# Even mixer: 64-row and 32-row tiles of the array in place of masked keys, and heads handled in pairs

## The chip, the cores and the metric

The kernel runs as one program on one core of one Trainium2 chip. The metric is the device time of one execution in microseconds (us). PE is the matrix engine (PEld its weight loads), DVE the vector engine, ACT the scalar engine, POOL the general engine, SP the engine that issues most DMAs. Each engine works through its own list of instructions in order.

## The reference, cut to what matters

Two blocks are computed on 256 tokens of width 1024 in float32: a first block of two layers, then a second block whose first layer is the *even mixer* (on 256 latent and 256 context tokens), followed by 16 experts, a second mixer and experts again. The change lies in the even mixer:

```python
q_a = rms_norm(heads_a(aq), na_qg) * HD_A ** -0.5          # 8 heads of 64
o_a = neighbourhood_attention(q_a, k_a, v, ck_a, cv_a, rpb) # latents: window + all context
co_a = block_attention(cq_a, ck_a, cv_a)                    # context queries: context keys
# mLSTM: 4 heads, keys and queries of 64, values of 128, once forward and once backward
Dm = where(causal, b_i - b_j + i_j, NEG);  m = max(a, Dm.max(-1))
h  = (exp(Dm - m) * (q k^T)) v / max(|den|, exp(-m))
out = concat([o_a, norm(h_f + h_b) * sigmoid(mo)]) @ w_out
```

## The kernel before, in words

All weight products are made exactly in float32 from two float32r parts (a high and a low one): three products of 128x128 by 128x256 for one, named `pt` (token-major) or `pf` (feature-major). ACT and DVE split each weight block of 1 MB into its parts (`wh`, `wl`). Small products (attention, transposes) run in float32; the profile records each of those as two instructions. PE's tile shape stands in the profile as rows*columns: 128*128 is the whole array, 64*128 its upper or lower half of rows, 128*64 one half of its columns.

The order of every engine's list is set before the run by a planner, from priorities, expected times and the time at which tiles come free. Tiles lie in pools beside each other in memory; the pools of the even mixer reuse the first block's memory, and a tile of the new pool can be written only when what lay there has been read.

The end of the first block: four chunks of the output product (`pt<-w,yT`), the squares of each chunk (`fjunk`, ACT), their sum (`fsum`, DVE), then on POOL 1/rms (`fnr`) and the 1/rms of the result (`fn2r`), `x<-xf` on DVE and ACT, and two diagonal matrices (`cT`). The even mixer needs its input feature-major: for the context tokens squares (`xn<-xc`), 1/rms (`nrme`, `nrmr` on POOL), diagonals `cT`, then eight blocks `htp` (PE) to `hfull` (ACT) to `hT`, `hTl` (DVE); for the latent tokens the same eight blocks from `fn2r`. Every `pt<-w,hT` needs them.

In the even mixer four mLSTM heads come first: `cmb` spreads the running maxima over the partitions (K = 64 rows, of which one counts), ACT makes the weights `E0` (forward) and `E1` (backward), `qk` is q k^T, DVE multiplies it in, `pom` is the product with v. The planner fills PE's waits there with the `pt` of the first four neighbourhood heads. Then `na_pair` runs for two pairs of heads, another `na_qkv` and the output gate follow, and `na_pair` for two more. In `na_pair`, `lgN` and `lgC` are logits, DVE finds minima and adds the bias, ACT makes exponentials, DVE divides, PE transposes (`ntp`), `poN` is the product with v, 64 columns of the array at a time. Two heads of 64 lie on the 128 partitions of one block of q and k. Since a product contracts all 128 partitions, the key tiles `mk` and `nkT` hold every head apart, with zeros on the other head's 64 partitions.

The PSUM tag `lg` (`cmb`, `qk`, `lgN`, `lgC`) has two buffers, `tp` two, `po` one. The pools of the even mixer lie in the order evenA0, evenA (which holds `mk`), evenC (`wmg`, then `xn`, `cT`, `hfull`, `nkT`, `cm`), evenB, evenD.

Of the kernel before, what the change touches and what calls it, by code (L numbers as in the profile page):

```python
# [10 lines left out]
F32 = mybir.dt.float32  # L11
# [48 lines left out]
# ---------------------------------------------------------------- constants of the shapes  # L60
# [174 lines left out]
class Emit:  # L235
# [29 lines left out]
    # ------------------------------------------------------------ small helpers  # L265
# [7 lines left out]
    def warm(self, where, tag="lg", after=None):  # L273
        """products that nothing reads, behind the latest one traced: they keep the tensor engine's clock up while it waits"""
# [62 lines left out]
    def stream(self, units):  # L337
        """units: weight blocks [128, 8, 256] in DRAM in the order of their use; each step yields one as the exact
        sum of two float32r parts, and has the next one split already"""
        nc = self.nc  # L340
        for n, u in enumerate(list(units) + [None] * AHEAD):
            if u is not None:
                h, lo = (self.ring.tile([P, KD, UW], F32R, tag=tag, name=tag, bufs=RING[tag]) for tag in ("wh", "wl"))
                w = self.ring.tile([P, KD, UW], F32, tag="w", name="w", bufs=RING["w"])
                # the first ones in pieces: nothing else can run yet
# [11 lines left out]
    def split(self, hi, lo, src, eng="v"):  # L357
        """src -> hi + lo exactly, both float32r"""
        self.nc.scalar.copy(hi, src)  # L359
        (self.nc.vector if eng == "v" else self.nc.gpsimd).tensor_tensor(out=lo, in0=src, in1=hi.bitcast(F32), op=ALU.subtract)  # L360

    def mm3(self, out, a, b):
        """out = sum over k of a_k^T b_k for lists of pairs (hi, lo) of float32r parts: the product of the two low
        parts lies below the last bit of float32"""
# [7 lines left out]
    def diag(self, r, d):  # L372
        """column r [128, 1] -> d: the diagonal matrix of it"""
        self.affine(d, self.cst["ident"], r, eng="s")
        return d

    def rms_diag(self, x, junk, d):
        """x [128, 1024] token-major -> d: the diagonal matrix of 1 / rms of its rows"""
# [9 lines left out]
    def features(self, xs, ds, hT, A, B=None, tok0=0, pool=None):  # L388
        """token tiles xs (list of [128, 1024] APs) scaled by the diagonal matrices ds -> A_k * x^T + B_k as the sum of
        hT[0] and hT[1] [128, k, tok0...]"""  # L390
# [16 lines left out]
    def features1(self, x, d, hT, A, B, tok0, pool):  # L407
        """features of one token tile, four blocks of columns at a time"""
# [12 lines left out]
    # ------------------------------------------------------------ set up  # L421
# [36 lines left out]
    # ------------------------------------------------------------ first block  # L458
# [26 lines left out]
    def proj_feat(self, w, hT, c0=0, nb=2, ntok=S, width=P, b0=0):  # L485
        """feature-major product: psum [width, nb * ntok] for the columns c0.. of the unit w"""
# [8 lines left out]
    def proj_tok(self, w, hT, t0=0, ntile=2):  # L495
        """token-major product: psum [128, ntile, 256] for the token tiles t0.."""
# [8 lines left out]
    def silu2(self, ps, pool, g):  # L505
        """psum -> g: 2 * silu"""
# [6 lines left out]
    def softmax_rows(self, nl, n, bias, pool, tag, bufs=3):  # L513
        """nl psum [128, n] negated logits (bias already negated, or None): returns exp tile and its row sums"""
# [15 lines left out]
    def p_transposed(self, p0, p1, pool):  # L530
        """p0 [128, 128], p1 [128, 256] -> sbuf [128 keys, (k0: q 0..255 | k1: q 128..255)]"""
# [12 lines left out]
    def first_layer(self, l, pool):  # L544
# [21 lines left out]
        # ---- latents, index weights, rope key, index key  # L566
# [45 lines left out]
        # ---- index queries, diff queries  # L612
# [8 lines left out]
        # ---- index scores and top 64  # L621
# [32 lines left out]
        # ---- MLA q, k, v  # L654
# [23 lines left out]
        # ---- diff keys, dsa queries  # L678
# [10 lines left out]
        # ---- diff and dsa values, MLA gate  # L689
# [8 lines left out]
        # ---- MLA attention  # L698
# [25 lines left out]
        # ---- dsa keys  # L724
# [7 lines left out]
        # ---- differential attention  # L732
# [53 lines left out]
        # ---- diff and dsa gates  # L786
# [17 lines left out]
        # ---- DSA attention  # L804
# [24 lines left out]
        # ---- short convolution  # L829
# [19 lines left out]
        # ---- out  # L849
# [8 lines left out]
    def final_squares(self, pool, c):  # L858
        """chunk c of x times the gain, and the sums of squares of both"""
# [13 lines left out]
    def final_norm(self):  # L873
        """x <- x / rms * gain; 1 / rms of the result goes to self.r2"""
# [33 lines left out]
    # ------------------------------------------------------------ modulation vectors  # L908
# [12 lines left out]
    def ada_chunks(self, pool):  # L921
        """the modulation products, 2048 columns at a time; yields after each quarter of such a product"""
# [28 lines left out]
    def mod_cols(self, l):  # L951
        """feature-major columns of shift and scale of the mixer: A [128, 2, 8], B [128, 2, 8] (lat, ctx)"""
# [13 lines left out]
    def router_prep(self, l, pool, tag):  # L966
        """router weights times the scale of the expert input, and what its shift adds to the logits"""
# [20 lines left out]
    def out_proj(self, yT, targets, pool, rwA):  # L988
        """targets: (first token tile of yT, [128, 2, 1024] to add to, gate tile, 0 for latents or 1 for context).
        The router's products of the new tokens and their squares are gathered on the way"""  # L990
# [30 lines left out]
    def head_norm(self, ps, nh, dh, pool, tag):  # L1021
        """psum [128, nh*dh] token-major -> sbuf, each head divided by its rms"""
# [11 lines left out]
    # ------------------------------------------------------------ even mixer  # L1034
    def even_mixer(self, l):
        nc, io, cst = self.nc, self.io, self.cst
        NT = 4
        with ExitStack() as ctx:
# [18 lines left out]
            # neighbourhood bias, negated, with the window  # L1057
# [3 lines left out]
            def bias_half(g):  # L1061
                G2r = T([P, 4, 6, 64], "nkT")
                for rr in range(2):
                    # [63 - qc, head, d, kc] -> head*465 + (5 + d - rr)*31 + 15 + kc - qc
# [14 lines left out]
            # ---- mLSTM v  # L1079
# [10 lines left out]
            # ---- gates  # L1090
# [61 lines left out]
            # ---- mLSTM q, k  # L1152
            mq = T([P, 2, 512], "mq")
            mk = T([P, 2, 2, 512], "mk")
# [5 lines left out]
            for b in range(2):  # L1160
                ps = self.proj_feat(w, hT, c0=b * P, nb=1, ntok=512)
                nc.vector.tensor_tensor(mk[:, b], ps[:, None].to_broadcast([P, 2, 512]),
                                        cst["gm2"].unsqueeze(2).to_broadcast([P, 2, 512]), op=ALU.mult)
            bias_flip(1, G2r)

            # ---- NA q, k, v of four heads
            # ---- mLSTM
# [5 lines left out]
            def eoff(d, t, i):  # L1173
                """column of block (tokens j in tile t, tokens i in tile i) in the packed weights"""
# [10 lines left out]
            for h in range(4):  # L1185
                b, j = h // 2, h % 2
                E = []
                for d in range(2):
                    ps = self.psum("lg", name="cmb")
                    self.mm(ps, cst["ident"][:64, 32 * d + h:32 * d + h + 1].to_broadcast([64, P]), cm, True, True)  # L1190
                    Ed = T([P, 10 * P], f"E{d}")
                    for t in range(NT):
# [3 lines left out]
                        # keep where token j <= i (forward) or j >= i (backward); j on partitions  # L1196
# [4 lines left out]
                for t in range(NT):  # L1201
                    lo = 0 if t < 2 else 256
                    ps = self.psum("lg", name="qk")
                    self.mm(ps[:, lo:512], mk[:, b, j, t * P:(t + 1) * P], mq[:, b, lo:512], True, True)
# [22 lines left out]
            def na_qkv(tags):  # L1227
                nkT = T([P, 2, 2, 512], tags[1])
                nc.gpsimd.memset(nkT[0:64, :, 1], 0.0)
                nc.gpsimd.memset(nkT[64:128, :, 0], 0.0)  # L1230
# [12 lines left out]
                for t in range(0, NT, 2):  # L1243
# [5 lines left out]
                    tv = tp.rearrange("p (t b s) -> p t b s", t=2, b=2)  # L1249
                    for j in range(2):  # L1250
                        pr = slice(64 * j, 64 * j + 64)
                        self.affine(nkT[pr, :, j, t * P:(t + 2) * P].rearrange("p b (t s) -> p t b s", t=2), tv[pr],
                                    self.vcol("nak")[pr], eng="vs"[j])
# [6 lines left out]
            # ---- output gate of the mLSTM  # L1260
# [8 lines left out]
            # ---- neighbourhood attention  # L1269
            def na_pair(hp, nqT, nkT, nv):  # L1270
                hb = hp % 2
                po = self.psum("po", name="poN")
                for j in range(2):
                    h = 2 * hp + j
                    # latent queries
                    PT = T([P, 4, 2, P], f"E{j}")
                    for qt in range(2):
                        ps = self.psum("lg", name="lgN")
                        self.mm(ps, nqT[:, hb, 256 + qt * P:256 + (qt + 1) * P], nkT[:, hb, j], True, True)
# [3 lines left out]
                        bias = G2[:, h, 2 - 2 * qt:6 - 2 * qt].rearrange("p a b -> p (a b)")  # L1283
# [3 lines left out]
                        sm = self.sm.tile([P, 1], F32, tag="smx", name="smx", bufs=8)  # L1287
                        nc.scalar.activation(p, ps, AF.Exp, bias=mn, scale=-1.0, accum_out=sm)
                        r = self.sm.tile([P, 1], F32, tag="smr", name="smr", bufs=8)
                        nc.vector.reciprocal(r, sm)  # L1290
                        nc.vector.tensor_scalar(p, p, r, None, op0=ALU.mult)
# [3 lines left out]
                        self.copy(PT[:, :, qt], tp.rearrange("p (a s) -> p a s", a=4))  # L1295
                    for kt in range(4):
                        self.mm(po[64 * j:64 * j + 64, 256:512], nv[:, kt, (2 * hb + j) * 64:(2 * hb + j + 1) * 64],
                                PT[:, kt].rearrange("p a s -> p (a s)"), kt == 0, kt == 3)
                    # context queries
                    PC = T([P, 2, 2, P], f"E{j}")  # L1300
# [768 lines left out]
```

## Time and profile before

| what | value |
| --- | --- |
| median of 3 runs | 1570.04 us (1568.9 to 1570.42) |
| profiled execution, span | 1568.5 us, mean granted PE clock 0.958 |
| PE busy in it | 1427.8 us (91%) |
| DVE, ACT, POOL busy | 719.7, 441.2, 161.6 us |
| even mixer, from the first `htp<-cT,xc` to the last `poN` | 417 to 700 us |

The profiled execution shows no time beside its span; the span lies 1.5 us under the median of the runs. Busy time of PE includes the tail of each pipelined product, so the starts of successive products tell PE's pace better than their durations.

### The profile page before, as it was taken

Reading aid. Unit: us, or ns where it says so; the run is one execution under the profiler, and the core shown is the slowest. Engines: PE = TensorE matmul, PEld = TensorE weight load, DVE = VectorE, ACT = ScalarE, POOL = GpSimd, SP = SyncE. Lnnn points to the kernel's source line nnn. Section 1 sums busy time; section 2 is a strip of 40 time slices with the busy share of each in tenths; the row PEclk is TensorE's granted clock in tenths of the full one; section 3 lists DMA queues with packets and bytes.
Section 4 is the critical chain, followed back from the end, with each engine's and each line's share of the span. In section 5 each row is a group of like instructions: output and inputs, shape, how many; then the busy total and the mean of one; then the engine's idle time right before and its main releaser. Section 6 shows DMA issues by size and latency. Waiting matters only on the chain.

```text
span 1568.5 us, 24539 instructions
## 1 busy us (share of the span) xinstructions
PE 1427.8 (91%) x10110; PEld 932.0 (59%) x10110; DVE 719.7 (46%) x1611; ACT 441.2 (28%) x883; POOL 161.6 (10%) x221
## 2 busy tenths in 40 slices
PE   8999999999999998989499999886549998999997
PEld 7576787767888885959333343332248785433342
DVE  4756544866654556365511111012166655433333
ACT  4334432444543324343111111102024432111110
POOL 2100120002101322000110000000143000000000
PEclk9999999999999999999799999998769998999999
DMA  7677665676623111114598888877533527999890
GB/s 292 231 297 271 237 244 175 235 291 229 233 65 93 53 34 63 68 66 187 207 360 324 326 294 307 336 301 298 195 128 109 221 85 305 421 421 418 331 378 30
DMA packets 65702, 359.22 MB, mean 229 GB/s; under 512 B 13027, under 2 KB 16349, under 8 KB 26793
## 3 DMA queue, kind: packets, MB, share of 16 engines
q1 hardware_dynamic: 57680, 335.04, 56.4%
q0 software_dynamic: 5824, 19.68, 3.8%
q10 hardware_dynamic: 2073, 2.79, 0.5%
q8 instruction: 84, 1.38, 0.4%
q14 instruction: 41, 0.34, 0.1%
HBM read 344.77 MB, written 12.71 MB: 228 GB/s over the span
## 4 chain that ended last, share of the span: by engine, by line
PE 37%; DMA 8%; DVE 2%; ACT 1%; issue 1%; POOL 1%; SPq 0%; ACTq 0%; POOLq 0%; DVEq 0%
PE ph L270 14%; PE py L270 6%; DMA w<-in_w_dram 5%; PE pt L270 4%; PE pq L270 3%; DMA ybuf<-ysq 2%; PE yc L270 2%; PE px L270 1%; PE gtp L284 1%; PE pyq L270 1%; PE lgG L270 1%; PE poG L270 1%; PE xtp L284 1%; DMA w<-in_odd_w_dram 1%; PE htp L270 0%
## 5 line engine op out<-in xcount | busy, mean ns | idle before, releaser
L270 PE MATMUL ph<-w,XT 128*64 128x512 f32 x1024 | 256.7, 617 | 30.1 <-DMA w<-in_w_dram 14.3
L360 DVE TENSOR_TENSOR wl<-w,wh 128x2048 fp32r<-128x2048 f32 (+2 forms) x74 | 152.1, 2058 | 103.3 <-ACT wh L359 103.1
L270 PE MATMUL pt<-wh,hT 128*128 128x256 f32 x640 | 185.6, 291 | 1.6 <-ACT hT L359 1.2
L270 PE MATMUL pt<-wl,hT 128*128 128x256 f32 x640 | 184.7, 289 | 1.8 <-DVE wl L360 1.7
L270 PE MATMUL pt<-wh,hTl 128*128 128x256 f32 x640 | 184.2, 291 | 0.2
L359 ACT CAST wh<-w 128x2048 fp32r<-128x2048 f32 (+2 forms) x74 | 127.1, 1718 | 136.3 <-PE pt L270 49.3
L270 PEld LDWEIGHTS ph<-w,XT 128*64 128x64 f32 x1024 | 70.3, 139 | 155.3 <-issue 127.1
L270 PE MATMUL pf<-hT,wh 128*128 128x256 f32 (+1 forms) x480 | 141.6, 299 | 0.3
L270 PE MATMUL pf<-hTl,wh 128*128 128x256 f32 (+1 forms) x480 | 141.5, 296 | 0.0
L270 PE MATMUL pf<-hT,wl 128*128 128x256 f32 (+1 forms) x480 | 140.5, 294 | 0.9 <-DVE wl L360 0.9
L1740 DVE SCALAR_TENSOR_TENSOR ga<-ga,ph 64x512 f32<-64x512 f32 x32 | 21.7, 679 | 234.7 <-ACT ga L1739 234.7
L270 PEld LDWEIGHTS pt<-wh,hT 128*128 128x128 f32 x640 | 122.7, 192 | 8.2 <-issue 3.6
L270 PEld LDWEIGHTS pt<-wl,hT 128*128 128x128 f32 x640 | 122.9, 192 | 6.9 <-issue 3.3
L270 PEld LDWEIGHTS pt<-wh,hTl 128*128 128x128 f32 x640 | 121.8, 191 | 7.1 <-issue 6.1
L270 PE MATMUL py<-w,gT 128*64 128x512 f32 x512 | 123.2, 603 | 1.3 <-DVE gT L1813 0.8
L270 PEld LDWEIGHTS pf<-hT,wh 128*128 128x128 f32 x480 | 91.7, 193 | 11.1 <-issue 4.7
L270 PEld LDWEIGHTS pf<-hT,wl 128*128 128x128 f32 x480 | 92.1, 192 | 7.2 <-issue 2.9
L270 PEld LDWEIGHTS pf<-hTl,wh 128*128 128x128 f32 x480 | 92.3, 192 | 5.5 <-issue 4.2
L270 PEld LDWEIGHTS py<-w,gT 128*64 128x64 f32 x512 | 37.4, 138 | 69.3 <-issue 66.7
L270 PE MATMUL ada<-w,cT 128*32 128x512 f32 x384 | 73.2, 612 | 1.0 <-DMA w<-in_ada_w_dram 1.0
L270 PE MATMUL pq<-w,XT 128*32 128x256 f32 x1024 | 71.8, 382 | 0.0
L270 PE MATMUL pt<-wh,yT 128*128 128x256 f32 x256 | 62.6, 289 | 0.0
(531 smaller groups left out, 2172.8 us busy)
## 6 DMA issues: line engine op xcount, KB each, us to landing
w<-in_w_dram SPq DMA_DIRECT2D x192, 1024.0 KB
w<-in_ada_w_dram SPq DMA_DIRECT2D x48, 1024.0 KB
w<-in_w_in_dram SPq DMA_DIRECT2D x30, 1024.0 KB
w<-in_even_w_dram SPq DMA_DIRECT2D x12, 1024.0 KB
w<-in_w_out_dram SPq DMA_DIRECT2D x8, 1024.0 KB
w<-in_even_out_dram SPq DMA_DIRECT2D x4, 1024.0 KB
ybuf<-ysb SPq DMA_DIRECT2D x16, 256.0 KB
w<-in_odd_w_dram SPq DMA_DIRECT2D x4, 1024.0 KB
```

What stands on the lines that cost most here:

```text
L270: self.last = self.nc.tensor.matmul(out, lhsT, rhs, start=start, stop=stop)
L284: self.nc.tensor.transpose(out, in_, self.cst["ident"][:k, :k])
L359: self.nc.scalar.copy(hi, src)
L360: (self.nc.vector if eng == "v" else self.nc.gpsimd).tensor_tensor(out=lo, in0=src, in1=hi.bitcast(F32), op=ALU.subtract)
L1740: nc.vector.scalar_tensor_tensor(g, g, 1.0, ph[0:n], op0=ALU.add, op1=ALU.mult)
```

## The change

It does five things in `even_mixer` (besides, comments and docstrings are gone from the whole file, so its line numbers differ):

1. `mk` becomes [128, 2, 512] and `nkT` [128, 2, 512], without zero halves; two masked products on DVE become copies, two half-height scalings per `nkT` step become one, and the four memsets of `nkT` go.
2. `qk`, `lgN` and `lgC` contract 64 partitions (row half j of the array for head j).
3. `cmb` contracts 32 partitions, rows 0 to 31 for the forward, 32 to 63 for the backward direction, and both stand before the work on either.
4. `na_pair` takes both heads of a pair together: two logit products one behind the other, and `poN` alternates between the heads (column halves of the array).
5. The pool evenA is 4 KB per partition shorter (`mk`), so evenC, evenB and evenD lie 4 KB lower. `wmg`, the first tile of evenC, now lies on one of the two buffers of `fjunk`.

```diff
-            mk = T([P, 2, 2, 512], "mk")
+            mk = T([P, 2, 512], "mk")
...
-                nc.vector.tensor_tensor(mk[:, b], ps[:, None].to_broadcast([P, 2, 512]),
-                                        cst["gm2"].unsqueeze(2).to_broadcast([P, 2, 512]), op=ALU.mult)
+                self.copy(mk[:, b], ps, "v")
...
-                E = []
+                E, cmb = [], [self.psum("lg", name="cmb") for _ in range(2)]
                 for d in range(2):
-                    ps = self.psum("lg", name="cmb")
-                    self.mm(ps, cst["ident"][:64, 32 * d + h:32 * d + h + 1].to_broadcast([64, P]), cm, True, True)
+                    r = slice(32 * d, 32 * d + 32)
+                    self.mm(cmb[d], cst["ident"][r, 32 * d + h:32 * d + h + 1].to_broadcast([32, P]), cm[r], True, True)
...
-                    self.mm(ps[:, lo:512], mk[:, b, j, t * P:(t + 1) * P], mq[:, b, lo:512], True, True)
+                    self.mm(ps[:, lo:512], mk[64 * j:64 * j + 64, b, t * P:(t + 1) * P], mq[64 * j:64 * j + 64, b, lo:512], True, True)
...
-                nkT = T([P, 2, 2, 512], tags[1])
-                nc.gpsimd.memset(nkT[0:64, :, 1], 0.0)
-                nc.gpsimd.memset(nkT[64:128, :, 0], 0.0)
+                nkT = T([P, 2, 512], tags[1])
...
+                PT = [T([P, 4, 2, P], f"E{j}") for j in range(2)]
+                for qt in range(2):
+                    lg = [self.psum("lg", name="lgN") for j in range(2)]
+                    for j in range(2):
+                        self.mm(lg[j], nqT[row[j], hb, 256 + qt * P:256 + (qt + 1) * P], nkT[row[j], hb], True, True)
+                    for j in range(2):
...
+                for kt in range(4):
+                    for j in range(2):
+                        self.mm(po[row[j], 256:512], nv[:, kt, (2 * hb + j) * 64:(2 * hb + j + 1) * 64],
+                                PT[j][:, kt].rearrange("p a s -> p (a s)"), kt == 0, kt == 3)
...
+                lg = [self.psum("lg", name="lgC") for j in range(2)]
+                for qt in range(2):
+                    for j in range(2):
+                        self.mm(lg[j][:, qt * S:(qt + 1) * S], nqT[row[j], hb, qt * P:(qt + 1) * P], nkT[row[j], hb, 0:256], True, True)
```

The order that the planner makes of it differs in two places that matter here. First ACT at the end of the first block; `xn,nrms<-xc` are the context squares, `cT` with `nrmr` the context diagonals, `x<-xf,fnr` the last step of the first block. Before:

```order
L381 ACTIVATE xn,nrms<-xc 128x1024
L359 CAST wh<-w 128x2048
L381 ACTIVATE xn,nrms<-xc 128x1024
L359 CAST wh<-w 128x2048
L305 ACTIVATE cT<-cpack,nrmr 128x128 x2
L871 ACTIVATE fjunk,fss<-x 128x256 x2
L871 ACTIVATE fjunk,fss<-xf 128x256 x2
L359 CAST wh<-w 128x2048
```

Of the change, from the last chunk's squares on (here POOL issues `wmg` and `gateb` and sets `cw` and `cm` behind `fn2r` and ahead of `nrme`; before, all that stood ahead of the final norm):

```order
L871 ACTIVATE fjunk,fss<-x 128x256 x2
L871 ACTIVATE fjunk,fss<-xf 128x256 x2
L305 ACTIVATE x<-xf,fnr 128x1024
L381 ACTIVATE xn,nrms<-xc 128x1024 x2
L305 ACTIVATE cT<-cpack,fn2r 128x128 x2
L305 ACTIVATE cT<-cpack,nrmr 128x128 x2
L305 ACTIVATE hfull<-htp,modc,modA 128x256 x16
```

The context squares have moved behind the first block's last step, and with them all sixteen `htp<-cT,xc` on PE behind the last `pt<-w,yT` (before, eight stood among these or right behind them, the rest among the first `pt<-w,hT`). Second PE in the third pair of neighbourhood heads (its logits read `mk` and `mq`, as those tags hold the second `na_qkv`). Before:

```order
L284 MATMUL ntp<-cpack,ne 128x128 x4
L270 MATMUL lgC<-mk,mq 128x256
L284 MATMUL ntp<-cpack,ne 128x128 x5
L270 MATMUL poN<-E_6756,nv_6441 64x256 x4
L270 MATMUL lgN<-mk,mq 128x512
```

Of the change:

```order
L270 MATMUL lgC<-mk,mq 128x256 x4
L284 MATMUL ntp<-cpack,ne 128x128 x8
L270 MATMUL poN<-E_6748,nv_6433 64x256
L270 MATMUL poN<-E_6749,nv_6433 64x256
L270 MATMUL poN<-E_6748,nv_6433 64x256
L270 MATMUL poN<-E_6749,nv_6433 64x256
...
L270 MATMUL lgN<-mk,mq 128x512
L284 MATMUL ntp<-cpack,ne 128x128 x5
L270 MATMUL lgN<-mk,mq 128x512
```

Here `poN` alternates between two heads, and `lgC` stands four in a row; of the sixteen `lgN` only the first four of this pair stand side by side, the others apart. The sixteen `qk` stand where they stood, each alone among `pt` or `pom`, and so do the eight `cmb`, of which two now enclose the transposes `cmT`.

## Rows read from the trace of the kernel before

**Rows 1.** Windows: stretch, length, busy of PE, PEld, DVE, ACT, POOL, PEclk, DMA
```profile
500.00:580.00 80.00, 80.00 (x590) 70.34 (x589) 44.48 (x124) 21.65 (x40) 23.57 (x41) 1.00 0.15 52
600.00:622.00 22.00, 19.05 (x83) 10.14 (x82) 18.07 (x50) 13.89 (x32) 7.03 (x10) 1.00 0.14 49
660.00:700.00 40.00, 36.49 (x184) 22.94 (x183) 27.07 (x77) 18.50 (x46) 2.56 (x2) 1.00 0.08 27
```

**Rows 2.** Timeline of PE, end of the first block: start, duration, engine, line, names, shape
```profile
423.01 0.83 PE L270 MATMUL htp<-cT,xc 128*128 128x128 f32 x6
...
429.19 0.28 PE L270 MATMUL pt<-wh,yTl 128*128 128x256 f32 x1
429.31 1.06 PE L270 MATMUL htp<-cT,xc 128*128 128x128 f32 x8
...
438.46 0.49 PE L270 MATMUL htp<-cT,x 128*128 128x128 f32 x2 [0.63 <-ACT cT L305]
...
462.55 0.81 PE L270 MATMUL g2f<-nkT,cpack 128*128 128x384 f32 x2
```

**Rows 3.** Timeline of ACT, the same stretch
```profile
402.09 1.05 ACT L381 ACTIVATE xn<-xc 128x1024 f32<-128x1024 f32 x1
...
435.62 1.16 ACT L305 ACTIVATE x<-xf,fnr 128x1024 f32<-128x1024 f32 x1
...
438.01 0.69 ACT L305 ACTIVATE cT<-cpack,fn2r 128x128 f32<-128x128 f32 x2 [0.59 <-POOL fn2r L312]
```

**Rows 4.** Timeline of POOL, the same stretch
```profile
398.94 0.64 POOL L1043 DMA_DIRECT2D wmg<-in_even_mg_dram  x1 [8.22 <-DVE ytmp L844]
...
400.37 0.55 POOL L1139 MEMSET cm<- 64x512 f32 x1
...
410.94 1.11 POOL L385 TENSOR_TENSOR nrmr<-nrme,neghalf 128x1 f32<-128x1 f32 x2
...
434.33 0.33 POOL L310 TENSOR_SCALAR fne<-fsum 128x2 f32<-128x2 f32 x1 [19.29 <-DVE fsum L877]
```

**Rows 5.** Timeline of DVE, the same stretch
```profile
433.66 0.49 DVE L404 CAST hT<-hfull 128x256 fp32r<-128x256 f32 x2
434.07 0.16 DVE L877 TENSOR_REDUCE fsum<-fss 128x4 f32<-128x16 f32 x1
```

**Rows 6.** Tile `hfull`, 424 to 452 us: count, duration ns min/median/max
```profile
L404 DVE CAST hT<-hfull x16: 277/294/296, 427.2 to 451.0; 128x256 fp32r<-128x256 f32 x16
L405 DVE TENSOR_TENSOR hTl<-hfull,hT x16: 408/426/427, 427.6 to 451.4; 128x256 fp32r<-128x256 f32 x16
```

**Rows 7.** Windows after the other idle stretch of PE, between the first block's layers
```profile
220.00:224.00 4.00, 0.72 (x7) 0.53 (x5) 2.29 (x1) 2.59 (x6) 2.50 (x4) 1.00 0.30 96
224.00:231.00 7.00, 6.60 (x29) 4.23 (x28) 1.40 (x3) 1.78 (x4) 4.44 (x7) 0.53 0.99 377
```

**Rows 8.** Timeline of PE around a `cmb` and a `qk`
```profile
519.42 0.28 PE L270 MATMUL pt<-wl,hT 128*128 128x256 f32 x1
519.63 1.12 PE L270 MATMUL cmb<-cm,cpack 64*128 64x512 f32 x2
520.68 0.38 PE L270 MATMUL pt<-wh,hTl 128*128 128x256 f32 x1
520.90 1.02 PE L270 MATMUL qk<-mq,mk 128*128 128x512 f32 x2
...
521.88 0.28 PE L270 MATMUL pt<-wl,hT 128*128 128x256 f32 x1
```

**Rows 9.** Timeline of PE: one head's `poN`, and the gate products on 32 columns
```profile
595.72 1.94 PE L270 MATMUL poN<-E,nv 128*64 128x256 f32 x8
...
465.47 0.40 PE L270 MATMUL mg<-hTl,wmg 128*32 128x128 f32 x8
```
**Rows 10.** Groups by line, PE: busy us, mean ns; of 600 to 622
```profile
L270 PE MATMUL poN<-E,nv 128*64 128x256 f32 x32 | 8.2, 389 | 0.1
```

**Rows 11.** The same, of 660 to 700
```profile
L270 PE MATMUL poN<-E,nv 128*64 128x256 f32 x47 | 11.9, 388 | 1.8 <-DVE E L291 1.0 <-ACT E L293 0.7
```

More of the change, by code (lines that the diff above doesn't have):

```diff
@@ L1186, in even_mixer @@
                 b, j = h // 2, h % 2
-                E = []
+                E, cmb = [], [self.psum("lg", name="cmb") for _ in range(2)]
                 for d in range(2):
-                    ps = self.psum("lg", name="cmb")
-                    self.mm(ps, cst["ident"][:64, 32 * d + h:32 * d + h + 1].to_broadcast([64, P]), cm, True, True)
+                    r = slice(32 * d, 32 * d + 32)
+                    self.mm(cmb[d], cst["ident"][r, 32 * d + h:32 * d + h + 1].to_broadcast([32, P]), cm[r], True, True)
+                for d in range(2):
+                    ps = cmb[d]
                     Ed = T([P, 10 * P], f"E{d}")
@@ L1248, in na_qkv @@
                         self.tr(tp[:, i * P:(i + 1) * P], kn[:, 2 * i:2 * i + 2].rearrange("p h d -> p (h d)"))
[L1249 to L1253, printed above, removed]
+                    self.affine(nkT[:, :, t * P:(t + 2) * P].rearrange("p b (t s) -> p t b s", t=2),
+                                tp.rearrange("p (t b s) -> p t b s", t=2, b=2), self.vcol("nak"))
                 w = W()
@@ L1272, in na_pair, with soft @@
                 po = self.psum("po", name="poN")
[L1273 to L1279, printed above, removed]
+                row = [slice(64 * j, 64 * j + 64) for j in range(2)]
+                def soft(p, ps, mn):
+                    sm = self.sm.tile([P, 1], F32, tag="smx", name="smx", bufs=8)
+                    nc.scalar.activation(p, ps, AF.Exp, bias=mn, scale=-1.0, accum_out=sm)
+                    r = self.sm.tile([P, 1], F32, tag="smr", name="smr", bufs=8)
+                    nc.vector.reciprocal(r, sm)
+                    nc.vector.tensor_scalar(p, p, r, None, op0=ALU.mult)
+                PT = [T([P, 4, 2, P], f"E{j}") for j in range(2)]
[4 more added lines that the diff above has]
+                    for j in range(2):
+                        ps = lg[j]
                         m0 = self.sm.tile([P, 1], F32, tag="mn", name="mn", bufs=8)
@@ L1282, in na_pair @@
                         mn = self.sm.tile([P, 1], F32, tag="mn2", name="mn2", bufs=4)
-                        bias = G2[:, h, 2 - 2 * qt:6 - 2 * qt].rearrange("p a b -> p (a b)")
+                        bias = G2[:, 2 * hp + j, 2 - 2 * qt:6 - 2 * qt].rearrange("p a b -> p (a b)")
                         nc.vector.tensor_tensor_reduce(ps[:, 256:512], ps[:, 256:512], bias, 1.0, m0, op0=ALU.add,
@@ L1286, in na_pair @@
                         p = T([P, 512], "ne", 3)
[L1287 to L1291, printed above, removed]
+                        soft(p, ps, mn)
                         tp = self.psum("tp", name="ntp")
@@ L1294, in na_pair @@
                             self.tr(tp[:, kt * P:(kt + 1) * P], p[:, kt * P:(kt + 1) * P])
[L1295 to L1300, printed above, removed]
-                    ps = self.psum("lg", name="lgC")
+                        self.copy(PT[j][:, :, qt], tp.rearrange("p (a s) -> p a s", a=4))
+                for kt in range(4):
+                    for j in range(2):
+                        self.mm(po[row[j], 256:512], nv[:, kt, (2 * hb + j) * 64:(2 * hb + j + 1) * 64],
+                                PT[j][:, kt].rearrange("p a s -> p (a s)"), kt == 0, kt == 3)
+                PC = [T([P, 2, 2, P], f"E{j}") for j in range(2)]
+                lg = [self.psum("lg", name="lgC") for j in range(2)]
+                for qt in range(2):
+                    for j in range(2):
+                        self.mm(lg[j][:, qt * S:(qt + 1) * S], nqT[row[j], hb, qt * P:(qt + 1) * P], nkT[row[j], hb, 0:256], True, True)
+                for j in range(2):
                     p = T([P, 512], "ne", 3)
                     for qt in range(2):
-                        s_ = ps[:, qt * S:(qt + 1) * S]
-                        self.mm(s_, nqT[:, hb, qt * P:(qt + 1) * P], nkT[:, hb, j, 0:256], True, True)
+                        s_ = lg[j][:, qt * S:(qt + 1) * S]
                         mn = self.sm.tile([P, 1], F32, tag="mn", name="mn", bufs=8)
                         nc.vector.tensor_reduce(mn, s_, axis=AX.X, op=ALU.min)
-                        sm = self.sm.tile([P, 1], F32, tag="smx", name="smx", bufs=8)
-                        nc.scalar.activation(p[:, qt * S:(qt + 1) * S], s_, AF.Exp, bias=mn, scale=-1.0, accum_out=sm)
-                        r = self.sm.tile([P, 1], F32, tag="smr", name="smr", bufs=8)
-                        nc.vector.reciprocal(r, sm)
-                        nc.vector.tensor_scalar(p[:, qt * S:(qt + 1) * S], p[:, qt * S:(qt + 1) * S], r, None, op0=ALU.mult)
+                        soft(p[:, qt * S:(qt + 1) * S], s_, mn)
                     tp = self.psum("tp", name="ntp")
@@ L1316, in na_pair @@
                             self.tr(tp[:, (2 * kt + qt) * P:(2 * kt + qt + 1) * P], p[:, qt * S + kt * P:qt * S + (kt + 1) * P])
-                    self.copy(PC, tp.rearrange("p (a b s) -> p a b s", a=2, b=2))
-                    for kt in range(2):
-                        self.mm(po[64 * j:64 * j + 64, 0:256], nv[:, kt, (2 * hb + j) * 64:(2 * hb + j + 1) * 64],
-                                PC[:, kt].rearrange("p a s -> p (a s)"), kt == 0, kt == 1)
+                    self.copy(PC[j], tp.rearrange("p (a b s) -> p a b s", a=2, b=2))
+                for kt in range(2):
+                    for j in range(2):
+                        self.mm(po[row[j], 0:256], nv[:, kt, (2 * hb + j) * 64:(2 * hb + j + 1) * 64],
+                                PC[j][:, kt].rearrange("p a s -> p (a s)"), kt == 0, kt == 1)
                 self.copy(yN[:, hp], po)
```

## Prediction

> **What bounds the kernel now.** I read the share of busy time first: PE works 91% of the span, so any time that PE loses where it never waits is lost to the end. Then the windows along the even mixer, to see where that holds. From 500 to 580 us PE is busy 80.00 of 80.00 us and no other engine above 45 [rows 1]: there an extra cycle of PE counts in full, and work saved on DVE, ACT or POOL counts nothing. In two stretches of neighbourhood heads PE has gaps: 600 to 622 (PE 19.05, DVE 18.07 of 22) and 660 to 700 (PE 36.49, DVE 27.07 of 40) [rows 1]. I then read the timelines of PE, ACT, POOL and DVE there (to see what PE waits for and what it fills the wait with), and PE's timeline around single small products, for what a change of tile shape costs.
>
> **The transition (term 1).** Before, the last `pt<-w,yT` starts at 429.19, and PE goes on at 429.31 with `htp<-cT,xc` [rows 2]: the context squares were done at 402 [rows 3], and `nrmr` at 412 [rows 4]. Until the latent features begin at 438.46 PE has 24 records of `htp<-cT,xc` and 18 `pt` to do, at paces of 0.112 us (0.83 us for six and 1.06 for eight: 0.115 a record) and 0.12: 2.7 + 2.1 = 4.8 us of work in 9.15. Eight more such records stood among the `pt<-w,yT` (0.9 us). From 438.46 to the first `g2f` at 462.55 it has 24.1 us of work without a pause [rows 2].
>
> In the changed order both squares stand behind `x<-xf` on ACT, and all sixteen `htp<-cT,xc` blocks behind the last `pt<-w,yT`. So nothing covers the final norm. The chain, step by step:
> - The `pt<-w,yT` end 0.9 us earlier, at 428.3. On DVE `fsum` takes the place of the two `hT` casts, which stand at 433.66 behind a weight split: 433.66 - 0.9 = 432.8, against 434.07 [rows 5].
> - `x<-xf` on ACT starts as much earlier, at 434.3 in place of 435.62, and lasts 1.16; the squares follow at 1.05 each [rows 3]: 437.5.
> - POOL has `fn2r` when `cT` may start. In before ACT's `cT` starts at 438.01 after a wait for it [rows 3], so 436.7 now. Behind it stand the issues of `wmg` and `gateb` (0.64 [rows 4] and, as I take it, the same), `cm` (0.55) and `cw` (half as many elements a partition, so about 0.28 as an estimate from `cm`'s row): 438.8. Then two `nrme` of the kind of `fne` (0.33 each) and `nrmr` (1.11 for two) [rows 4]: 440.6.
> - The context `cT` and the first `htp<-cT,xc`: 438.01 to 438.46 was that step [rows 2, 3], so 441.0.
>
> PE stands still from 428.4 to 441.0, 12.6 us, and has the same work before it: 24.1 + 4.8 + 0.9 = 29.8 us. `g2f` then begins at 470.8, against 462.55: +8.3. The start adds about 0.5, since the first block needs `hfull`, `hT` (0.29) and `hTl` (0.43) [rows 6] before the first `pt`; later DVE makes a block in 0.72 us and PE uses one in 48 or 96 `pt`, so it keeps ahead. Last the clock: between the first block's layers PE was busy only 0.72 of 4 us, and in the 7 us behind that the granted clock was 0.53, half of 2.4 GHz [rows 7]. That costs 7.00 x (1 - 0.53) = 3.3 us there; I take 2.4, as the start has its own waits which a slow clock fills. Sum +8.3 + 0.5 + 2.4 = **+11**. Lower bound +7.5 (ACT done sooner, no clock loss); upper bound +14 (clock as in rows 7, and a wait of POOL for its DMA issue: 8.22 us of waiting stand at `wmg`'s row, though that was for memory). PE is full from there to 600, so all of it is passed on; the experts behind 700 load their weights as memory comes free, later by as much.
>
> **Single `qk` on half the rows (term 2).** Before, `qk` streams through the whole array among `pt`: from 520.90 to 521.88 stand two records of 512 columns and one `pt` (its row left out), 0.98 us. A `cmb` on 64 rows has the same columns, and from 519.42 to 520.90 stand two `pt` and its two records: 1.48 [rows 8]. Less one `pt` (0.113, the pace here) that is 1.37, so going to 64 rows and back costs 0.39 us. The sixteen `qk` now do the same, each alone between products on the whole array, all in the stretch where PE has no gap [rows 1]: 16 x 0.38 = **+6** (between 0, if the 0.39 belongs to `cmb`'s broadcast weights, and +6.4). Halving the rows streams no fewer columns, so it gives nothing back.
>
> **`cmb` on 32 rows (term 3).** The eight `cmb` pay their 0.39 already. Four times the transposes `cmT` (64 rows) now stand between two `cmb` of 32 rows, so there may be one more change of shape a head, without a wait for the big products: 4 x 0.1 = **+0.4** (0 to 4 x 0.39 = 1.6). The Trainium skill, "TensorEngine Tiling (Array Packing)", Key Properties, says "Mode switching requires drain: changing tiling mode (not just tile) drains the TensorE"; rows 8 agree for 128 to 64 rows, at 0.39 us, and by that rule a change from 32 to 64 rows would cost as well, so this term would be 1.6. Both `cmb` now hold both `lg` buffers; `qk` waits for ACT to have read one, but PE has `pt` to do.
>
> **Neighbourhood heads, 600 to 622 (term 4).** PE has 32 records of `poN` [rows 10] at 0.22 apart (1.94 us for eight, less the tail [rows 9]), beside logits and transposes. Alternating column halves can run beside each other: the gate products on 32 columns take 0.40 us for eight records of 128 columns [rows 9], where eight `htp` of as many columns take 1.06 [rows 2]. So `poN` falls from 7.0 to 3.5 us. DVE's 18.07 of 22 change little (minima, bias and sums stay), so of the 3.5, and of pairs of logits, I take **-2**: between -3.9 (all of it and the pairs, if DVE's waits shrink too) and +1.4 (four changes of shape at 0.35, DVE the bound).
>
> **Neighbourhood heads, 660 to 700 (term 5).** 48 records of `poN` (47 in the trace, one missing [rows 11]) at 0.216: 10.4, of which half, 5.2, can go. `lgC`: 16 records (four a head, by the code) of 256 columns at half of a `qk` record's 0.43 [rows 8], 3.4, half 1.7. `lgN`: only four of the sixteen records stand side by side, 4 x 0.43 and the likes behind, 1.7 if their neighbours join. Sum -8.6, against eight changes to half rows and back at 0.38, +3.0: -5.6. PE has 3.5 us of waits there that don't shrink, and may get more: **-4**, between 0 and -8.6. No row of before shows two products on different row halves at once, only on column parts. The Trainium skill, the same page, Theoretical Speedup, gives "Up to 2×" for a dimension of 64 or less; by it the logits would give their whole 3.4, without it the term is about -2.
>
> **Costed at nothing.** The copies in place of masked products, half the scalings of `nkT` and the memsets lie on DVE, ACT and POOL, where PE is full [rows 1]. If that cover went, DVE's 0.7 us a pair would count.
>
> **Sum.** +11 + 6 + 0.4 - 2 - 4 = +11.4. The profiled execution has a span of 1568.5 us, 1.5 below the median of the runs, so 1570.0 + 11.4 = 1581 us.
>
> **Rivals.**
> - *Tile shapes cost `qk` nothing.* For: the 0.39 stands on `cmb` alone, whose weights are a broadcast column. Against: any wait for the array to empty would show just there. Then +11 + 0 - 2 - 7 (no changes in the pairs): +2, to +5 with half of it: 1574. Chance 0.12.
> - *The hole is short.* The squares wait behind `x<-xf` by order only; if POOL's issues run off in no time and PE's clock stays up, term 1 is +5, the sum also with smaller gains +6: 1576. Against: rows 3 and 4 give every step. Chance 0.15.
> - *Faster.* PE, and not the chain of DVE and ACT, limits both stretches of neighbourhood heads, and all pairs overlap: 96 `poN` at 0.216 fall from 20.7 to 10.4, `lgN` (32 at 0.43) from 13.7 to 6.9, `lgC` from 6.9 to 3.4: -20.7, against +17.4 of terms 1 to 3: -3.3, 1566.7. It decides as soon as the pairs give more than 17.4. For: PE's 36.49 of 40. Against: most `lgN` stand apart in PE's order, and DVE's 18.07 of 22. Chance 0.05.
> - *The pairs don't pair:* `poN` waits at each step for the other head's exponentials, terms 4 and 5 are +1 and 0: +18, 1588. Chance 0.10.
>
> The forecast itself has 0.58; its own range is 1576 to 1587. The range for 8 in 10 takes in most of the rivals at both ends: 1573 to 1590. This kernel's times tell a difference of 0.2% (3.1 us) from none. Faster by over that has the faster rival's chance, with a smaller rest 0.05; within it lie half of the first rival: 0.07; slower 0.88.
>
> **What would show it.** In the profile after: PE idle some 12 us between the last `pt<-w,yT` and the first `htp<-cT,xc`, the granted clock near 0.5 in the us behind that, and `g2f` near 473; each `qk` about 0.4 us longer from the `pt` ahead of it to the second one behind; a group of 16 alternating `poN` in about half of 16 x 0.22; 600 to 622 shorter by 2, 660 to 700 by 4. I am wrong if `htp<-cT,xc` starts soon after the last `pt<-w,yT`, or if the neighbourhood heads give back more than the transition and the `qk` cost.

## The result and the profile after

The changed kernel takes 1583.4 us (median of 4 runs, 1581.95 to 1585.49), the kernel before 1570.23 in the same comparison: ratio 1.0099, 95% interval 1.0079 to 1.0119. (The ratio is an estimate of its own and not the quotient of the two medians, which is 1.0084 and lies in the interval: by the medians the change costs 13.2 us, by the ratio 15.5.) The forecast was 1581, in the range 1573 to 1590. The profiled execution has a span of 1579.9 us and a mean granted clock of 0.948.

PE at the end of the first block: last product of `yT`, first transposes of the context, first `g2f` (the rows that answer to [rows 2]):

```profile
425.16 0.28 PE L270 MATMUL pt<-wh,yTl 128*128 128x256 f32 x1
...
436.58 2.08 PE L270 MATMUL htp<-cT,xc 128*128 128x128 f32 x8 [11.15 <-ACT cT L305]
...
469.21 1.13 PE L270 MATMUL g2f<-nkT,cpack 128*128 128x384 f32 x3
```

PE stands still for 11.15 us, waiting for ACT's `cT`. From the last `pt<-w,yT` to `g2f` it is 44.05 us, where it was 33.36 [rows 2]: 10.7 more, of which 0.9 is the eight `htp` records that moved in, so the hole costs 9.8. (425.16 lies 4.0 us before 429.19. Beside the 0.9, 3.1 of that were gained in the first block, which the change doesn't touch, and belong to no term: in the trace of `qk` alone, below, where every engine has the order of before, the last `pt<-w,yT` also starts 2.8 us earlier, at 426.43.) ACT and POOL show the chain behind the wait, in the order in which the prediction walked it:

```profile
430.95 1.15 ACT L305 ACTIVATE x<-xf,fnr 128x1024 f32<-128x1024 f32 x1 [1.97 <-POOL fnr L312]
432.01 1.04 ACT L381 ACTIVATE xn<-xc 128x1024 f32<-128x1024 f32 x1
...
433.05 1.04 ACT L381 ACTIVATE xn<-xc 128x1024 f32<-128x1024 f32 x1
...
436.13 0.93 ACT L305 ACTIVATE cT<-cpack,nrmr 128x128 f32<-128x128 f32 x2 [1.37 <-POOL nrmr L385]
```

```profile
432.86 0.65 POOL L1043 DMA_DIRECT2D wmg<-in_even_mg_dram  x1
...
434.92 0.53 POOL L383 TENSOR_SCALAR nrme<-nrms 128x1 f32<-128x1 f32 x2
435.52 1.11 POOL L385 TENSOR_TENSOR nrmr<-nrme,neghalf 128x1 f32<-128x1 f32 x2
```

The squares end at about 434.1, but `nrme` can start only at 434.92, behind POOL's two DMA issues and two memsets: POOL ends last, as forecast. The windows (columns as in [rows 1]) show what the clock did there and in the two stretches of neighbourhood heads:

```profile
428.00:441.00 13.00, 4.19 (x18) 3.89 (x19) 4.13 (x8) 7.18 (x18) 6.08 (x14) 0.54 0.67 156
441.00:450.00 9.00, 9.00 (x73) 9.00 (x73) 6.21 (x18) 4.51 (x8) 0.00 (x0) 0.90 0.01 2
...
620.00:640.00 20.00, 16.52 (x86) 9.52 (x85) 15.24 (x42) 8.91 (x22) 5.25 (x9) 0.91 0.25 83
...
680.00:700.00 20.00, 18.48 (x89) 10.83 (x88) 15.54 (x46) 9.06 (x25) 1.27 (x1) 0.91 0.16 53
```

Behind the hole PE runs at the lower level, 1.2 GHz: eight `htp` take 2.08 us, where they took 1.06 [rows 2]. The granted clock also fell in the stretches of the heads, 0.91 of 20 us twice, where it was 1.00 [rows 1].

A `qk` and the products around it, and then logits and `poN`, in PE's timeline:

```profile
580.44 0.28 PE L270 MATMUL pt<-wl,hT 128*128 128x256 f32 x1
580.65 1.12 PE L270 MATMUL qk<-mq,mk 64*128 64x512 f32 x2
581.70 0.39 PE L270 MATMUL pt<-wh,hTl 128*128 128x256 f32 x1
581.92 0.28 PE L270 MATMUL pt<-wh,hT 128*128 128x256 f32 x1
...
593.07 1.12 PE L270 MATMUL lgN<-nkT,nqT 64*128 64x512 f32 x2
...
607.42 1.13 PE L270 MATMUL lgC<-nkT,nqT 64*128 64x256 f32 x4
...
616.07 1.94 PE L270 MATMUL poN<-E,nv 128*64 128x256 f32 x14
...
673.54 1.13 PE L270 MATMUL lgN<-mk,mq 64*128 64x512 f32 x4
...
677.68 1.79 PE L270 MATMUL lgN<-mk,mq 64*128 64x512 f32 x4 [0.29 <-ACT ne L1276]
```

From 580.44 to 581.92 are two `pt` and one `qk`: 1.48 us, the figure that [rows 8] gave for a `cmb` on 64 rows. `poN` does fourteen records in the 1.94 us in which it did eight [rows 9]: the column halves run side by side. The row halves can too: at 673.54 four `lgN` records take 1.13 us, at 593.07 two take 1.12. But that is the only place where they do so in full. In three other groups one head's records begin only behind most of the other's, as in the next four `lgN`, which take 1.79 us. The four `lgC` of 607.42 are one head's, on one row half, one after another.

### The profile page after: what moved, and what is told of

Same layout as the page of the kernel before. It is cut to its first block, busy times and chain, and to the rows that moved or that the text cites. A ratio compares the mean times of both kernels' runs of the same rounds, so it can differ in the third digit from the quotient of the medians.

```text
span 1579.9 us, 24534 instructions
## 1 busy us (share of the span) xinstructions
PE 1437.1 (91%) x10110; PEld 931.7 (59%) x10110; DVE 718.9 (46%) x1609; ACT 440.1 (28%) x881; POOL 150.9 (10%) x217
## 4 chain that ended last, share of the span: by engine, by line
PE 37%; DMA 9%; DVE 2%; ACT 1%; issue 1%; POOL 0%; SPq 0%; ACTq 0%; POOLq 0%; DVEq 0%
PE ph L270 14%; PE py L270 6%; DMA w<-in_w_dram 5%; PE pt L270 4%; PE pq L270 3%; DMA ybuf<-ysq 2%; PE yc L270 2%; PE px L270 1%; PE gtp L284 1%; PE pyq L270 1%; PE poG L270 1%; PE lgG L270 1%; PE xtp L284 1%; DMA w<-in_odd_w_dram 1%; PE htp L270 0%
## 5 line engine op out<-in xcount | busy, mean ns | idle before, releaser
L270 PE MATMUL ph<-w,XT 128*64 128x512 f32 x1024 | 260.4, 625 | 27.5 <-DMA w<-in_w_dram 13.1
```

The source lines that it names most:

```text
L270: self.last = self.nc.tensor.matmul(out, lhsT, rhs, start=start, stop=stop)
```

## The experiments

All times are medians; ratios are to the kernel before, run on the same chip in the same comparison. Differences of two ratios are given with the root of the sum of the squares of their half intervals. Several answers that the times leave open are in the traces, stage by stage; they stand in a table at the end of this section (the *stage table*).

**The changed kernel in the old layout.**

```diff
-            mk = T([P, 2, 512], "mk")
+            mk = T([P, 2, 2, 512], "mk")[:, :, 0]
```

> The changed kernel with mk (and the second nkT, which takes its place) allocated at the old size of 8 KB, half of it unused, so that wmg, xn and the rest lie where they lay before; shapes and pairs as changed. Theory (the hole at the transition comes from the new addresses alone and is passed on): the hole goes, htp<-cT,xc follows the last pt<-w,yT at once, about 1583.4 - 10 = 1573 us. Rival (the hole has another cause, or the experts absorb it): 1583 us.

1569.22 us, ratio 1.0018 (1.0000 to 1.0036): 0.0081 +- 0.0027 below the change, 13 +- 4 us. The theory holds. The hole is gone, and from the `pt` shown here to the first `g2f`, at 459.38, it is 33.36 us, as before:

```profile
426.02 0.28 PE L270 MATMUL pt<-wh,yTl 128*128 128x256 f32 x1
426.14 1.06 PE L270 MATMUL htp<-cT,xc 128*128 128x128 f32 x8
```

**The hole alone, in the kernel before.** Here `nv1` moves to another pool, so that evenC slides down 4 KB.

```diff
-{"evenA": ("mq", "mk", "E0", "E1", "hn", "nv1", "G2"), "evenD": ("ne", "hsq", "hraw")}
+{"evenA": ("mq", "mk", "E0", "E1", "hn", "G2"), "evenD": ("ne", "hsq", "hraw", "nv1")}
```

> The kernel before with one tile (nv1, 4 KB) moved from the pool evenA to evenD, so that evenC begins at 147264, 1 KB inside the first block's pool, as in the changed kernel; no product and no shape differs. ACT's context squares come behind x<-xf, as in the change. Theory (the hole alone costs what the trace of the changed kernel shows between the last pt<-w,yT and g2f): +10.3, about 1578.5 us. Rival (the hole is made up for later): 1569 us.

1579.39 us, ratio 1.0058 (1.0040 to 1.0076): +9 us (6.3 to 11.9), from the addresses that one tile moved. PE's timeline has the same wait as the change, and from its last `pt<-w,yT` (425.42) to the first `g2f` (469.28) it is 43.86 us, 10.5 more than before, 0.9 of it the eight records that moved in:

```profile
436.84 2.08 PE L270 MATMUL htp<-cT,xc 128*128 128x128 f32 x8 [11.14 <-ACT cT L305]
```

**How much overlap it takes.** A pad of 1024 bytes in place of 4096.

> The changed kernel with mk (and the second nkT) only 1 KB a partition longer, so that evenC begins at 148288, the byte at which the first block's pool with xf and fjunk ends; with 960 bytes the order of all engines stays that of the change, with 1024 ACT's context squares stand early again. Theory (it is the overlap with that pool, by 1 KB of 4, that makes the hole): as the old layout, about 1569 us. Rival (the 4 KB matter in another way): 1583 us.

1574.35 us, ratio 1.0048 (1.0034 to 1.0061). The hole is gone, as from the old layout:

```profile
427.85 1.06 PE L270 MATMUL htp<-cT,xc 128*128 128x128 f32 x8
```

So it is an overlap with the first block's memory that sets the order; with 960 bytes of pad, which leave `wmg` 64 bytes inside the old pool, the squares keep their late place (an order alone, not run). Two causes fit: that the planner starts a new pool's work only when the last work on an overlapped pool, here `x<-xf`, is issued, or that it is the one buffer of `fjunk` on which `wmg` lies. No run here tells them apart. Yet the time is 0.0030 +- 0.0023 above that of the 4 KB pad, which neither theory expected. In its profile the clock fell to 0.76 in a stretch of the heads, where it stayed at 1.00 from 600 to 700 with the 4 KB pad:

```profile
480.00:500.00 20.00, 20.00 (x84) 14.48 (x84) 11.81 (x15) 7.89 (x14) 2.40 (x8) 0.91 0.30 95
620.00:640.00 20.00, 19.18 (x106) 13.46 (x106) 10.94 (x28) 5.14 (x14) 2.96 (x6) 0.76 0.17 54
```

A granted clock of 0.76 over 20 us is 4.8 us of full speed; the heads took 126.07 us in this trace and 122.82 with the 4 KB pad (cut as in the stage table), 3.3 more. The order of PE differs a little between the two pads; why the clock falls with one and not with the other stays open.

**`qk` on half the rows, alone, in the kernel before.**

```diff
-mk[:, b, j, t * P:(t + 1) * P], mq[:, b, lo:512]
+mk[64 * j:64 * j + 64, b, j, t * P:(t + 1) * P], mq[64 * j:64 * j + 64, b, lo:512]
```

> The kernel before with one line changed: qk contracts 64 rows (half j of the same masked tile). The order of every engine is the same, word for word. Theory: 16 x 0.38 = +6, about 1576 us. Rival (the change of shape costs nothing): 1570 us.

1574.18 us, ratio 1.0038 (1.0024 to 1.0052): +6.0 us (3.8 to 8.2) with the order of every engine unchanged. The theory holds.

**`qk` on all rows again, in the changed kernel of old layout.** `mk` has its zero halves back, `cmb` and the heads stay as changed.

> The run before it in this list, and mk again with zero halves and qk on all 128 rows; cmb on 32 rows and the neighbourhood heads as changed. Theory (each lone qk on half the rows costs 0.38 us, sixteen of them 6 us): 6 us under the kernel with the old layout, about 1567 us. Rival (the change of shape is hidden or cheap): as that kernel, 1573 us.

1568.94 us, ratio 1.0000 (0.9987 to 1.0014): 0.0018 +- 0.0023 below the kernel with the old layout, which leaves both theories standing (6 us would be 0.0038). The run before settles it, and the traces agree. The stretch with the `qk` is 3.8 us shorter here (113.06 against 116.87 in the stage table), at a lower granted clock, 0.98 against 1.00. The clock was lower in most of these runs, 0.947 to 0.956 over the whole execution against 0.949 to 0.959: the runs at 0.949 to 0.952 took 1567.21 to 1572.44 us with `qk` on all rows and 1575.16 to 1576.29 on half. What lowers the clock isn't shown.

**`cmb` on 32 rows, alone, in the kernel before.**

> The kernel before with cmb alone on 32 rows (0 to 31 or 32 to 63), each where the planner puts it. Theory (cmb pays for a change of shape already, cmT makes one more): +0.4, within 0.2% of before, 1569 us. Rival (the two changes of shape of every cmb are dearer): +2 us, 1571 us.

1569.46 us, ratio 1.0006 (0.9992 to 1.0020): by the times no difference that can be measured; +0.4 fits and +2 isn't excluded. In the stage table the stretch with all eight `cmb` is 0.3 us longer, which excludes the +2 there. It is the one place where `cmT` stands between two `cmb`. PE's timeline of it, in this run and then before:

```profile
492.83 1.12 PE L270 MATMUL cmb<-cm,cpack 32*128 32x512 f32 x2
493.88 0.46 PE L284 MATMUL cmT<-cpack,cm 64*128 64x64 f32 x4
494.27 1.12 PE L270 MATMUL cmb<-cm,cpack 32*128 32x512 f32 x2
495.32 1.56 PE L270 MATMUL g2f<-nkT,cpack 128*128 128x384 f32 x4
```

```profile
494.95 0.46 PE L284 MATMUL cmT<-cpack,cm 64*128 64x64 f32 x4
495.25 1.93 PE L270 MATMUL cmb<-cm,cpack 64*128 64x512 f32 x4
497.11 1.24 PE L270 MATMUL g2f<-nkT,cpack 128*128 128x384 f32 x3
```

Each step of the two `cmb` is 1.05 us (492.83 to 493.88, 494.27 to 495.32), the same as from 519.63 to 520.68 in [rows 8], where the next product was on the whole array. Before, `cmT` and both `cmb` shared one stay on 64 rows, 2.16 us to the next `g2f` (494.95 to 497.11); now it is 2.49 (492.83 to 495.32). So two more changes of shape cost 0.33 us.

**Pairs alone, logits on all rows, in the kernel before.** `na_pair` is the changed one but for the operands:

```diff
-self.mm(lg[j], nqT[row[j], hb, ...], nkT[row[j], hb], True, True)
+self.mm(lg[j], nqT[:, hb, ...], nkT[:, hb, j], True, True)
```

> The kernel before with only na_pair changed: heads in pairs, poN alternating, but lgN and lgC on all 128 rows with the masked keys. Theory (poN halves, but PE then waits for DVE and ACT; the changes of shape of lgN and lgC are gone): 2 to 5 us under before, 1565 to 1568 us. Rival (the stretches are bound by DVE and ACT alone): 1570 us. Rival (PE bound, all of poN's 10 us comes back): 1560 us.

1558.86 us, ratio 0.9946 (0.9932 to 0.9960): 8.5 us faster (6.3 to 10.7), more than the theory and near the second rival, in which PE bounds both stretches and all of `poN`'s 10 us comes back. In the traces the heads are 10.5 us shorter (118.24 against 128.73).

**The same with logits on half the rows.** The edit is the last one, the other way round, with the masked keys kept.

> The kernel before with na_pair in pairs, as in the earlier run of pairs on full rows (1558.9 us), but lgN and lgC on 64 rows of the same masked keys. Theory (each group of logits on half the rows costs a change of shape and back, and few of them overlap): about 6 us over the full rows, 1565 us. Rival (the changes of shape fall into PE's waits there): 1559 us. Rival (the halves run side by side): 1555 us.

1566.10 us, ratio 0.9980 (0.9966 to 0.9994): 0.0034 +- 0.0020 above the full rows, 5 +- 3 us (7.2 by the medians). The theory holds, and both rivals fall: on half the rows the logits take back a good part of what the pairs give. The lower clock of this run's profile (0.95 in the heads, where all rows had 1.00) is not the whole of it: two of these runs at a mean clock of 0.955 took 1565.53 and 1567.05 us, and the six on all rows, at 0.954 to 0.957, took 1555.88 to 1562.17.

**Pairs on full rows, `poN` head by head.**

```diff
-for kt in range(4):
-    for j in range(2):
+for j in range(2):
+    for kt in range(4):
         self.mm(po[row[j], 256:512], ...)
```

> The kernel before with na_pair in pairs on full rows, but poN head by head, not alternating between the column halves. Theory (the 10 us that the pairs gave are poN's two column halves running side by side, 96 x 0.216 / 2 = 10.4): back to about 1569 us. Rival (they come from the order, two heads' logits ahead of the transposes): 1559 us.

1566.77 us, ratio 0.9989 (0.9978 to 1.0000): 0.0043 +- 0.0018 above the alternating one, so 7 +- 3 us of the 8.5 are the two column halves side by side; the rest, 2 us, would be the order (1.5 in the stage table, at a clock of 0.99). Two heads now take two times 1.94 us where the alternating kernel's fourteen records take 1.94. First without, then with alternation:

```profile
595.04 1.94 PE L270 MATMUL poN<-E,nv 128*64 128x256 f32 x8
598.60 1.94 PE L270 MATMUL poN<-E,nv 128*64 128x256 f32 x8
```

```profile
598.47 1.94 PE L270 MATMUL poN<-E,nv 128*64 128x256 f32 x14
...
601.79 0.65 PE L270 MATMUL poN<-E,nv 128*64 128x256 f32 x2
```

**The head that is late goes first.** The last row shows two records alone: the planner issues a head's product as soon as it can, and the rest later. With `for j in (1, 0)` it waits for the later head and issues sixteen at once.

> Pairs on full rows as in the run that took 1558.9 us (0.9946 of before), but poN alternates beginning with the second head, whose exponentials come last, so that the planner puts all 16 (and all 8) records in one group in place of a first product alone and the rest behind it. Theory (each group costs a change of shape and back, 0.3 us on column halves, and a lone product overlaps with nothing): 8 groups fewer, 2 us less, 1557 us, ratio 0.993. Rival (PE has waits there anyway): 1559 us.

1557.53 us, ratio 0.9929 (0.9904 to 0.9955): faster than both kernels by a clear margin, but the times can't tell it from the run of pairs on full rows (0.0017 +- 0.0029 below). The traces can: at a clock of 1.00 in both, the heads take 116.35 us here and 118.24 there, 1.9 less, as the theory has it. The groups are as meant:

```profile
599.59 1.95 PE L270 MATMUL poN<-E,nv 128*64 128x256 f32 x16
```

**The stages in the traces.** Times of whole executions scatter by several us, but a trace can be cut at the same products in every run. The first stretch goes from the first `g2f` to the last `qk` and holds nearly all the `qk` and all the `cmb`. The second goes from there to the first `pt` behind the last `poN` and holds all the neighbourhood heads, with the same 765 records of PE in every trace (761 without alternation). The clock is the mean granted one. Each row is one execution; where neither the stretch nor the clock differs from before, the stretches repeat within 0.05 us.

| trace | first stretch, us | clock | second stretch, us | clock |
| --- | --- | --- | --- | --- |
| before | 111.09 | 1.00 | 128.73 | 1.00 |
| the hole alone | 111.10 | 1.00 | 128.68 | 1.00 |
| `qk` on half the rows, alone | 116.67 | 1.00 | 129.09 | 1.00 |
| `cmb` on 32 rows, alone | 111.37 | 1.00 | 128.72 | 1.00 |
| pairs, logits on all rows | 111.10 | 1.00 | 118.24 | 1.00 |
| the same, late head first | 111.10 | 1.00 | 116.35 | 1.00 |
| the same, no alternation | 111.09 | 1.00 | 127.21 | 0.99 |
| pairs, logits on half the rows | 111.09 | 1.00 | 126.90 | 0.95 |
| the change | 116.95 | 1.00 | 125.21 | 0.97 |
| the change in the old layout | 116.87 | 1.00 | 122.82 | 1.00 |
| the same, `qk` on all rows | 113.06 | 0.98 | 124.17 | 0.99 |

The second stretch before, with pairs on all rows, in the old layout and in the change (columns as in [rows 1]):

```profile
573.64:702.37 128.73, 119.52 (x767) 91.80 (x765) 74.83 (x196) 49.86 (x107) 19.03 (x20) 1.00 0.15 51
...
571.38:689.62 118.24, 110.84 (x767) 89.09 (x765) 72.87 (x192) 47.93 (x104) 19.18 (x20) 1.00 0.16 55
...
576.25:699.07 122.82, 115.37 (x767) 87.54 (x766) 73.24 (x191) 47.20 (x103) 15.03 (x18) 1.00 0.16 53
...
586.16:711.37 125.21, 118.52 (x766) 89.05 (x765) 73.51 (x191) 47.41 (x103) 14.65 (x18) 0.97 0.15 52
```

At a clock of 1.00, `qk` on half the rows costs 5.6 us in the first stretch and 0.4, the last one's, in the second. Pairs on all rows give 10.5. The old layout has the heads of the change: its 122.82 is 4.6 above pairs on all rows, and without the last `qk`'s 0.4 the half rows take 4.2.

## Why the prediction was right, term by term

**The transition, forecast +11.** Right in mechanism and size: 9.8 in the trace, +9 and 13 in the two runs that add or remove it. The chain came out step by step (POOL last, behind issues and memsets). The stand-still was 11.15 us rather than 12.6: `fn2r` was there at 432.86, 0.7 us sooner than I had read from ACT's wait (436.7 less the 3.1 of the first block), and POOL's items follow each other a little faster than their durations add up. Of the 44.05 us, 11.4 go to the stand-still and the `pt` ahead of it and 29.8 to the work that I counted; the 2.8 left are the start and the clock, for which I took 0.5 and 2.4. The rival "the hole is short" falls.

**Single `qk`, forecast +6.** Right: +6.0 alone, by the runs and by the stage table, and 1.48 us in the timeline. The rival "tile shapes cost `qk` nothing" falls: the 0.39 of [rows 8] was not `cmb`'s broadcast weights.

**`cmb`, forecast +0.4.** The size was right, by luck. The prediction has `cmT` between two `cmb` four times, at 0.1 us each, as a change without a wait; in the order it stands there once, and that place costs 0.33 us. The Trainium skill, "TensorEngine Tiling (Array Packing)", Key Properties, says that changing the tiling mode drains the engine. The traces agree: 0.39 us from 128 rows to 64 and back [rows 8], 0.37 (6.0 / 16) in the run of `qk` alone, and 0.33 for the two more changes between 32 and 64 rows. So a change between two small shapes is hardly cheaper here; there is only one such place.

**Neighbourhood heads, forecast -2 and -4.** The sign was right, and the size came out by two errors that met. In the two profiles the last `qk` starts 12.5 us later after than before (586.16 against 573.64), the first `lgN` of the third pair 12.7 later (673.54 against 660.87) and the first `pt` behind the last `poN` 9.0 later (711.37 against 702.37). That is +0.1 (0.4 of it the last `qk`'s) and -3.7, so the sign "shorter by 2" did not show. The lower clock there (0.91 twice, 3.6 us of full speed by 0.09 x 20 x 2) was in no term; in the old layout, with the same heads at a clock of 1.00, it is -1.0 (again with the `qk`'s 0.4) and -4.9.

First, I held DVE and ACT to bound the stretches and discounted `poN`'s gain. The run of pairs alone shows that PE was on the path: 10.5 us in its trace (8.5 by the runs), as much as the 10.4 of `poN`, though 1.5 to 2 of it is the order. Second, I counted eight changes to half rows and back in one stretch (3.0 us), and four in the other only in its bound. PE's timeline of the change has nine and eleven stays on 64 rows, sixteen of the twenty with one head's product alone. At 0.38 us each that would be 7.6; the traces show 4.2, so the count prices them too high, and where the rest is hidden isn't shown. And of the overlap that I credited to `lgN` and `lgC` (1.7 each) only the four records at 673.54 happened in full. The number of stays could have been counted in the changed order. The Trainium skill, the same page, Theoretical Speedup, gives "Up to 2×" for a dimension of 64 or less. `poN` and the `lgN` at 673.54 agree; here only products that stand next to each other on different tiles get it.

**Sum.** Hole +9, `qk` +6, `cmb` +1, pairs -8.5, half logits +5: +13 us (+- 5) from the single runs, against 13.2 measured by the medians. The two profiles add up as well: -4.0 up to the last `pt<-w,yT`, +10.7 to `g2f`, +5.9 to the last `qk`, -3.5 in the heads and +2.4 behind them make the 11.4 by which the spans differ, within rounding. Of the first, 0.9 is the hole's; the other 3.1 belong to no term, and neither do the 2.4 at the end, where the granted clock was 0.92 against 0.93. The rival "faster" was right that PE, more than the chain of DVE and ACT, limits the heads, but it needed `lgN` and `lgC` to overlap too, and one group of four did in full. The rival in which `poN` waits for the other head falls with its fourteen records in 1.94 us.

## What to carry to other kernels

A part of the array saves time only when its neighbour in the engine's order works on another part: count the stays on a small tile in the final order, price each alone at a change of shape and back (here an upper bound: 7.6 us by the count, 4.2 in the traces), and take the smaller tile only where the pairs win. Here the fastest version keeps the zero halves, uses column halves for the products with v, alternates them, and starts with the head that is ready last (this last step is 1.9 us by the traces, and too small for the times). A tile that becomes smaller moves all that lies behind it: look at which old memory the next one now touches before looking at the products.

## What the runs showed of the hardware

Records on two column halves that alternate run side by side in float32: sixteen in 1.95 us, eight of one head in 1.94. Two row halves do the same (four `lgN` records in 1.13 us, two in 1.12). The granted clock fell not only behind the hole (0.54 from 428 to 441) but also within stretches where PE changes shape and waits: in the run of pairs with half logits it was 0.76 and 0.91 in windows of 20 us,

```profile
600.00:620.00 20.00, 18.32 (x69) 9.60 (x70) 16.12 (x42) 11.30 (x25) 6.76 (x10) 0.76 0.22 78
...
660.00:680.00 20.00, 17.77 (x87) 11.06 (x85) 14.70 (x41) 9.47 (x23) 1.28 (x1) 0.91 0.15 53
```

and in that with full rows 1.00 in both. Half rows alone don't make it fall: the change in the old layout has the same heads and 1.00 from 600 to 700. What does, no run here settles.
